# One decoder layer in fp32 on one core: subtractions moved to GpSimd, raw memory results, heads by the bank and x loaded ahead in a blocked-product kernel

## The chip, the core and the metric

The kernel runs on one core of one Trainium2 chip. A core has TensorE (PE, matrix products), VectorE (DVE), ScalarE (ACT) and GpSimd (POOL), which work side by side on tiles in SBUF, and PSUM banks of 128 x 512 fp32 values into which TensorE writes. Each engine takes its instructions in the order of its own queue. SyncE (SP) and GpSimd issue the DMA transfers. The metric is the device time of one execution in microseconds; less is better.

## The reference

One layer of a hybrid decoder: 512 tokens, width 2048, fp32. One normed input goes through one projection to three groups of heads, whose results are normed, gated and projected back; then follows a two-layer MLP with squared ReLU. Cut to what matters:

```python
def gla_chunked(q, k, v, log_a):          # 8 heads, 64 query/key and 128 value columns
    def step(state, xs):
        qi, ki, vi, gi = xs
        b = jnp.cumsum(gi, axis=2)
        inter = jnp.einsum('bhck,bhkv->bhcv', qi * jnp.exp(b), state)
        rel = b[:, :, :, None, :] - b[:, :, None, :, :]
        decay = jnp.exp(jnp.where(causal, rel, -jnp.inf))
        scores = jnp.einsum('bhik,bhijk,bhjk->bhij', qi, decay, ki)
        intra = jnp.einsum('bhij,bhjv->bhiv', scores, vi)
        ...

def reference(x, mem, ...):
    xn = rms_norm(h, attn_norm_g)
    proj = xn @ w_in
    (gq, gk, gv, gg, ga, fq, fk, fv, fg, ff, mq, mg) = jnp.split(proj, _split_points(), axis=-1)
    gla_o = gla_chunked(heads(gq), heads(gk), heads(gv), log_sigmoid(...) / 16)
    fox_o = forgetting_attention(rms_norm(fq), rms_norm(fk), fv, log_f)      # 4 heads, causal
    mk, mv = jnp.split(rms_norm(mem, mem_norm_g) @ w_mem_kv, 2, axis=-1)     # 256 memory tokens
    m_p = softmax(rms_norm(mq) . rms_norm(mk) / sqrt(128))
    mem_o = m_p . mv                                                          # 4 heads
    o = rms_norm(concatenate([gla_o, fox_o, mem_o]))
    gate = concatenate([silu(gg), sigmoid(fg), sigmoid(mg)])
    h = x + (o * gate) @ w_out
    u = relu(rms_norm(h, mlp_norm_g) @ w_up)
    return h + (u * u) @ w_down
```

## The kernel before

**Products.** Each fp32 matrix product is made of three matmuls in a reduced format (`mm3`, lines 154 to 156): the high half of one side by the high and the low half of the other, and the low half by the high. A block of weights comes by DMA, ScalarE casts it to its high half and VectorE subtracts that from it for the low half (line 370 in the blocked products, 146 and 147 in the plain projections).

**Blocked products.** Large projections are computed by the scheme of seven products for a 2 x 2 block matrix, in the order 1, 5, 6, 3, 7, 2, 4 (`multiply`, line 374). The right-hand sides for products 5, 6, 7 and 4 are differences of weight blocks. `Weights.prepare` makes them in place with `minus` (line 332, on VectorE), and `split` halves them. The left-hand sides (`left0` to `left6`) are sums of blocks of the activations. A product 6 adds to the accumulators of product 1, and so waits until the result of product 1 has been added to its part of the output. Three variants follow one another:

- `Pair` (lines 465 to 510): the projections gv and fq, fk, in four pairs in00, in01, in10 and in11 of seven products each, from 96 to 254 us. Its blocks are 128 x 1024, its `minus` (line 481) stands on GpSimd for products 7 and 4 and on VectorE for 5 and 6.
- `out0` and `out1` (from 735 to 910 us): the output projection. `out0` is the `w_first` of the code; its first splits are made while the last gates are. `block` (line 977) loads the part of x that a product is added to, `after` (line 988) adds the product to it.
- the MLP, up and down (910 to 2183 us), which the change leaves alone.

**Between the pairs and the output projection**, from 254 to 735 us, run the small projections, GLA, FoX (forgetting attention), memory attention and the gates. GLA takes the tokens in four chunks of 128. For each chunk it makes seven score groups, one for each level of halving (`lp_128` to `lp_2`): two differences of the cumulated decay against a reference row (lines 672 and 673, 128 x 256 each), an exponential on ScalarE, the products with queries (678) and keys (683), four matmuls (686) and a masked copy out of PSUM into the scores (690). Each level waits for the one step of each kind before it. Between them TensorE is fed with matmuls of fv, mq and the memory projection mkv, which the scheduler puts there. `attend` (line 402) is the softmax attention of FoX and memory, head by head.

**Order.** The program is written down in sequence and a scheduler orders each engine's instructions by priority: a block in `tc.high_priority(offset=...)` comes ahead by that amount. The weights use `AHEAD` = 3000, GLA uses 300, x of out0 and out1 uses 300. GpSimd's queue also carries the transfers of the left-hand sides to DRAM (`oo`, line 918), which are fetched back and halved anew (`resplit`, lines 858 and 859). The masks of GLA (`tri`, `suf`, `cmask`, `lmask`, lines 524 to 557) are built on GpSimd during the pairs.

Of the kernel before, what the change touches and what calls it, by code (L numbers as in the profile page):

```python
# [32 lines left out]
FH = 4  # L33
# [13 lines left out]
def hybrid_layer(  # L47
# [252 lines left out]
    class Weights:  # L300
# [30 lines left out]
        def minus(self, p, dst, a, b):  # L331
            V.tensor_sub(dst, a, b)  # L332
# [69 lines left out]
    def attend(n, logits, rowmax, v, dst, name):  # L402

        av = abank(f"av_{name}")
        sm = tp.tile([128, 4], F32, tag=f"sm{name[0]}", name=f"sm_{name}", bufs=2)
        nmx = tp.tile([128, 4], F32, tag="nmx", name=f"nmx_{name}", bufs=2)
        for h in range(4):
            lg = abank(f"lg_{name}_{h}")
            logits(h, lg)
            src = rowmax(h, lg, nmx[:, h : h + 1])  # L410
            p = tmp(f"p_{name}_{h}", "tb")
            A.activation(
                p[:, : n * 128], src[:, : n * 128], AF.Exp, bias=nmx[:, h : h + 1], accum_out=sm[:, h : h + 1]
            )
            pT = abank(f"pT_{name}_{h}")
            for s in range(n):
                T.transpose(pT[:, s * 128 : s * 128 + 128], p[:, s * 128 : s * 128 + 128], ident)
            pTs = tmp(f"pTs_{name}_{h}", "tc")
            A.copy(pTs[:, : n * 128], pT[:, : n * 128])
            for s in range(n):  # L420
                T.matmul(
                    av[:, h * 128 : h * 128 + 128], lhsT=pTs[:, s * 128 : s * 128 + 128], rhs=v(s, h),
                    start=s == 0, stop=s == n - 1,
                )
        rc = tp.tile([128, 4], F32, tag="hr", name=f"rc_{name}", bufs=4)
        V.reciprocal(rc, sm)
        V.tensor_mul(heads4(dst), heads4(av), rc.unsqueeze(2).broadcast_to([128, 4, 128]))
# [38 lines left out]
    class Pair(Weights):  # L466
# [13 lines left out]
        def minus(self, p, dst, a, b):  # L480
            (G if p in (7, 4) else V).tensor_tensor(dst, a, b, op=ALU.subtract)
# [143 lines left out]
    for ql in qls:  # L625
        G.memset(ql, 0.0)
    state = tmp("state", "rbx")
    fqT = bigt(2, [128, 4, S], "fqT")
    fkT = bigt(3, [128, 4, S], "fkT")
    with tc.high_priority(offset=GLA_AHEAD):  # L630
        for t in range(NT):
            normed_T(o[:, t, 1024:1536], g_fq, FOX_SCALE, fqT[:, :, t * 128 : t * 128 + 128], f"fq{t}")
        for c in range(NT):
# [31 lines left out]
            for li, B in enumerate(LEVELS):  # L665
# [6 lines left out]
                V.tensor_sub(ev[:, :, :hb], ref, bv[:, :, :hb])  # L672
                V.tensor_sub(ev[:, :, hb:], bv[:, :, hb:], ref)
# [33 lines left out]
            if c:  # L707
                qe = tmp(f"qe_{c}", "tc")
                V.tensor_mul(qe, qT, eb)
            ops = [abank(f"o_{c}_{i}") for i in range(2)]  # L710
            for h in range(GH):
                p, s = h // 2, (h % 2) * 64
                dst = ops[h % 2][:, p * 128 : p * 128 + 128]
                if c:
                    T.matmul(
                        dst, lhsT=qe[s : s + 64, p * 128 : p * 128 + 128],
                        rhs=state[s : s + 64, p * 128 : p * 128 + 128], start=True, stop=False,
                    )
                T.matmul(dst, lhsT=sc[:, h, :], rhs=o[:, c, h * 128 : h * 128 + 128], start=c == 0, stop=True)
# [31 lines left out]
    mqT = bigt(0, [128, 4, S], "mqT")  # L751
    for t in range(NT):
        scaled(o[:, t, 1536:2048], ps[t], rs_x(t), t)
        normed_T(o[:, t, 1536:2048], g_mq, FOX_SCALE, mqT[:, :, t * 128 : t * 128 + 128], f"mq{t}")

    mps = [[gbank(f"mkv_{m}_{n}") for n in range(2)] for m in range(MT)]

    room = spare[:, : 6 * M].rearrange("p (i m) -> p i m", m=M)
    macc = room[:, 0, :]
    for k in range(NK):  # L760
        with tc.high_priority(offset=AHEAD):
            mt = room[:, 1 + k % 3, :]
            nc.sync.dma_start(mt, memT[k])
            mh, ml = (tp.tile([128, M], FR, tag=f"mem{p}", name=f"mem{p}_{k}") for p in "hl")
            split_gain(mt, g_mem[:, k : k + 1], mh, ml)
            add_squares(macc, mt, k == 0, f"mem{k}", room[:, 4 + k % 2, :])
# [6 lines left out]

    with tc.high_priority(offset=AHEAD):
        mrstd = token_rstd(macc, MT, "mem")
# [4 lines left out]
    for m in range(MT):  # L780
        mk = tmp(f"raw_mk{m}", "ta")
        scaled(mk, mps[m][0], mrstd[:, m : m + 1], m)
        normed_T(mk, g_mk, 1.0, mkT[:, :, m * 128 : m * 128 + 128], f"mk{m}")
        with tc.high_priority(offset=AHEAD):
            A.activation(mv[:, m, :], mps[m][1], AF.Copy, scale=mrstd[:, m : m + 1])
# [21 lines left out]
    for t in reversed(range(NT)):  # L807
        n = (t + 1) * 128

        def fox_logits(h, lg, t=t, n=n):  # L810
            T.matmul(
                lg[:, :n], lhsT=fqT[:, h, t * 128 : t * 128 + 128], rhs=fkT[:, h, :n], start=True, stop=False
            )
            T.matmul(
                lg[:, :n], lhsT=negid[:, h : h + 1].broadcast_to([32 + FH, 128]), rhs=rows_r[:, :n],
# [3 lines left out]
        def fox_max(h, lg, nmx, t=t, n=n):  # L819
            ls = tmp(f"ls_{t}_{h}", "ta")  # L820
            V.tensor_tensor_reduce(
                ls[:, :n], lg[:, :n], cmask[:, S - n :], 1.0, 0.0, ALU.add, ALU.max, accum_out=nmx
            )
            V.tensor_scalar(nmx, nmx, -1.0, None, op0=ALU.mult)
            return ls
# [49 lines left out]
    def mem_max(h, lg, nmx):  # L875
        V.tensor_reduce(nmx, lg[:, :M], AX.X, ALU.max, negate=True)
        return lg

    for n, (group, silu) in enumerate(gates):
# [42 lines left out]
        if n == 0:  # L922
            with tc.high_priority(offset=AHEAD):
                for t in range(NT):
# [3 lines left out]
                            lg[:, :M], lhsT=mqT[:, h, t * 128 : t * 128 + 128], rhs=mkT[:, h, :], start=True, stop=True  # L928
# [45 lines left out]
    def out_pair(n):  # L974
        z, ht = {}, {}

        def block(r, c):

            with tc.high_priority(offset=300):
# [277 lines left out]
```

## Time and profile before

| | |
|---|---|
| median of three runs | 2185.28 us (2185.14 to 2186.91) |
| profiled execution: time, span | 2185.21 us, 2183.5 us |
| TensorE busy | 2126.2 us, 97% |
| VectorE, ScalarE, GpSimd busy | 1631.3, 1123.2, 213.0 us |
| TensorE's clock over the span | 0.993 of full speed |

A row of the profile's waits names who waited, for what, and gives total us, how often, and the longest. A row of the timeline gives the start and the length of an instruction in us, its engine, line, operation, and its output and inputs with their shapes; a last bracket is idle time ahead of it. A row of windows gives the width of a stretch, then for each engine the busy us (and instructions), the granted clock of TensorE, the DMA share and GB/s. Tile names stand without buffer numbers, so `raw_in` is any pair's weight block and `spare` a working area that holds others.

### The profile page before, as it was taken

What the parts mean: (1) busy time and instruction counts of PE and PEld (TensorE: products, weight loads), DVE (VectorE), ACT (ScalarE), POOL (GpSimd) and SP (SyncE); (2) the same over time, 40 slices, a digit from 0 to 9 for tenths busy, and PEclk for the clock granted to TensorE, in tenths of its full rate; (3) what the DMA queues carried; (4) which work ended last, traced back from release to release, by engine and by line L of the source; (5) the groups of instructions that cost most, each with busy time, mean ns of one, the idle gap of its engine ahead of it and who ended that gap; (6) DMA issues with size and microseconds to landing.
All of it is one profiled execution on the core that took longest, in us unless ns stands there. A gap on an engine that the chain in (4) does not pass through costs nothing.

```text
span 2183.5 us, 25488 instructions
## 1 busy us (share of the span) xinstructions
PE 2126.2 (97%) x9746; PEld 1728.5 (79%) x9746; DVE 1631.3 (75%) x1800; ACT 1123.2 (51%) x1535; POOL 213.0 (10%) x245
## 2 busy tenths in 40 slices
PE   8999999989999889999999999999999999999999
PEld 7887777767777668878888888888788788788787
DVE  6579977884666779887768768769868767877875
ACT  6454433344564545755554555556646545556443
POOL 1346100000000003100000000000000000000000
PEclk9999999999999989999999999999999999999999
DMA  7333211241213455533543443455577678668654
GB/s 269 102 118 112 87 59 49 88 143 39 88 61 132 180 217 212 211 117 141 177 144 137 167 168 120 162 182 193 195 219 203 183 202 248 168 191 253 182 167 131
DMA packets 74628, 339.24 MB, mean 155 GB/s; under 512 B 8633, under 2 KB 10681, under 8 KB 53002
## 3 DMA queue, kind: packets, MB, share of 16 engines
q1 hardware_dynamic: 55898, 270.76, 35.3%
q0 software_dynamic: 18608, 66.86, 11.7%
q8 instruction: 76, 1.25, 0.2%
q14 instruction: 46, 0.38, 0.1%
HBM read 266.54 MB, written 71.04 MB: 155 GB/s over the span
## 4 chain that ended last, share of the span: by engine, by line
PE 78%; DVE 11%; DMA 4%; issue 3%; ACT 2%; POOL 1%; SPq 0%; DVEq 0%; ACTq 0%; POOLq 0%
PE acc_up L154 9%; PE acc_up L155 9%; PE acc_up L156 9%; PE acc_dn L155 7%; PE acc_dn L156 7%; PE acc_dn L154 7%; PE acc_out L154 2%; PE acc_out L155 2%; PE acc_out L156 2%; DMA left1l<-op 2%; DVE hl_dn L370 1%; DVE raw_dn L332 1%; DMA left5l<-op 1%; PE gg L154 1%; PE ut L1072 1%
## 5 line engine op out<-in xcount | busy, mean ns | idle before, releaser
L370 DVE TENSOR_TENSOR hl_up<-raw_up,hl_up 128x1024 fp32r<-128x1024 f32 x224 | 271.6, 1221 | 141.6 <-ACT hl_up L370 141.5
L370 ACT CAST hl_up<-raw_up 128x1024 fp32r<-128x1024 f32 x224 | 235.3, 1052 | 253.7 <-PE acc_up L156 193.9
L370 DVE TENSOR_TENSOR hl_dn<-raw_dn,hl_dn 128x1024 fp32r<-128x1024 f32 x224 | 270.5, 1221 | 99.5 <-ACT hl_dn L370 98.7
L370 ACT CAST hl_dn<-raw_dn 128x1024 fp32r<-128x1024 f32 x224 | 234.4, 1053 | 204.6 <-PE acc_dn L156 163.5
L332 DVE TENSOR_TENSOR raw_dn<-raw_dn,raw_dn 128x2048 f32<-128x2048 f32 x64 | 146.1, 2286 | 16.1 <-DMA raw_dn<-in_w_down_dram 15.9
L332 DVE TENSOR_TENSOR raw_up<-raw_up,raw_up 128x2048 f32<-128x2048 f32 x64 | 145.1, 2267 | 1.4 <-DMA raw_up<-in_w_up_dram 1.3
L370 ACT CAST hl_out<-raw_out 128x1024 fp32r<-128x1024 f32 x56 | 58.7, 1052 | 68.6 <-PE acc_out L156 55.3
L1172 POOL DMA_DIRECT2D hd<-m x48 | 41.0, 854 | 516.1 <-ACT m L1171 516.1
L370 DVE TENSOR_TENSOR hl_out<-raw_out,hl_out 128x1024 fp32r<-128x1024 f32 x56 | 69.2, 1253 | 25.0 <-ACT hl_out L370 25.0
L1171 ACT COPY m<-acc_dn 128x512 f32<-128x512 f32 x96 | 54.5, 587 | 30.3 <-PE acc_dn L156 30.3
L1064 POOL DMA_DIRECT2D op<-u x32 | 17.1, 534 | 486.3 <-ACT u L1073 479.1
L370 DVE TENSOR_TENSOR hl_hl_in<-spare,hl_hl_in 128x1024 fp32r<-128x1024 f32 x31 | 45.6, 1481 | 15.6 <-ACT hl_hl_in L370 15.6
L154 PE MATMUL gg<-ahi_x,hl_gg 128*128 128x512 f32 x128 | 54.6, 427 | 2.6 <-ACT raw_mk L222 2.2
L370 ACT CAST hl_hl_in<-spare 128x1024 fp32r<-128x1024 f32 x31 | 32.5, 1049 | 43.4 <-PE acc_in L156 18.9
L155 PE MATMUL acc_dn<-hl_dn,left 128*128 128x512 f32 x128 | 50.3, 393 | 4.6 <-DVE hl_dn L370 4.6
L155 PE MATMUL gg<-alo_x,hl_gg 128*128 128x512 f32 x128 | 53.7, 419 | 0.0
L156 PE MATMUL gg<-ahi_x,hl_gg 128*128 128x512 f32 x128 | 53.2, 415 | 0.0
L154 PE MATMUL acc_up<-hl_up,left 128*128 128x512 f32 x128 | 49.9, 390 | 3.1 <-ACT z L1127 3.1
L155 PE MATMUL acc_in<-hl_hl_in,sh 128*128 128x512 f32 x128 | 50.2, 392 | 2.6 <-DVE hl_hl_in L370 2.6
L155 PE MATMUL acc_dn<-hl_dn,left0h 128*128 128x512 f32 x128 | 50.2, 392 | 1.2 <-DVE hl_dn L370 1.2
L154 PE MATMUL acc_in<-hl_hl_in,sh 128*128 128x512 f32 x128 | 49.9, 390 | 0.7 <-DVE o L499 0.7
L155 PE MATMUL acc_dn<-hl_dn,left3h 128*128 128x512 f32 x128 | 50.5, 395 | 0.0
(566 smaller groups left out, 6320.0 us busy)
## 6 DMA issues: line engine op xcount, KB each, us to landing
raw_up<-in_w_up_dram SPq DMA_DIRECT2D x64, 1024.0 KB, 4.8
raw_dn<-in_w_down_dram SPq DMA_DIRECT2D x64, 1024.0 KB, 6.8
hd<-m POOLq DMA_DIRECT2D x48, 512.0 KB, 5.6
raw_out<-in_w_out_dram SPq DMA_DIRECT2D x16, 1024.0 KB, 5.7
op<-u POOLq DMA_DIRECT2D x32, 512.0 KB, 3.8
op<-s POOLq DMA_DIRECT2D x24, 512.0 KB, 2.9
spare<-in_w_pair_dram SPq DMA_DIRECT2D x16, 512.0 KB, 4.3
raw_in<-in_w_pair_dram SPq DMA_DIRECT2D x16, 512.0 KB, 3.6
```

The lines of the kernel that those rows point to most:

```text
L154: T.matmul(ps, lhsT=ah, rhs=bh, start=start, stop=False, skip_group_check=on)
L155: T.matmul(ps, lhsT=ah, rhs=bl, start=False, stop=False, skip_group_check=on)
L156: T.matmul(ps, lhsT=al, rhs=bh, start=False, stop=stop, skip_group_check=on)
L332: V.tensor_sub(dst, a, b)
L370: made = A.copy(hi, part), V.tensor_sub(lo, part, hi.bitcast(F32))
L1064: nc.gpsimd.dma_start(down_op[c][i][:, half * 1024 : half * 1024 + 1024], tile)
L1072: T.transpose(tps[:, m * 128 : m * 128 + 128], z[:, t * 512 + m * 128 : t * 512 + m * 128 + 128], ident)
L1171: A.copy(st[:, t * 512 : t * 512 + 512], acc[t])
L1172: nc.gpsimd.dma_start(dst, st.rearrange("p (t n) -> p t n", t=2), accum_op=ALU.add)
```

## The change

Seven edits in one.

1. The differences for product 5 of the pairs go from VectorE to GpSimd, so that GpSimd has 5, 7 and 4.
2. In `out0`, the differences for products 7 and 4 go from VectorE to GpSimd.
3. GLA's two differences a level go from VectorE to GpSimd.
4. The queries that GLA multiplies with the state are written into a zeroed tile with one head's rows and zeros in the other's, and the matmul takes all 128 rows.
5. The results of the memory projection are copied out of PSUM unscaled, with their scale applied after; the norms of the memory queries come after the memory keys' instead of before the projection.
6. `attend` takes as many heads at once as fit in a bank: one exponential per head still, but one maximum, one copy and one transposed bank for 2 to 4 heads in the small blocks.
7. The parts of x for `out0` are loaded at priority 3 x AHEAD instead of 300.

```diff
         def minus(self, p, dst, a, b):
-            V.tensor_sub(dst, a, b)
+            (G if self.name == "out0" and p in (7, 4) else V).tensor_tensor(dst, a, b, op=ALU.subtract)
...
-        for h in range(4):
-            lg = abank(f"lg_{name}_{h}")
-            logits(h, lg)
-            src = rowmax(h, lg, nmx[:, h : h + 1])
+        m, b = n * 128, 4 // n
+        for h0 in range(0, 4, b):
+            lg = abank(f"lg_{name}_{h0}")
+            for i in range(b):
+                logits(h0 + i, lg[:, i * m : i * m + m])
+            src = rowmax(h0, b, lg, nmx[:, h0 : h0 + b])
...
         def minus(self, p, dst, a, b):
-            (G if p in (7, 4) else V).tensor_tensor(dst, a, b, op=ALU.subtract)
+            (G if p in (5, 7, 4) else V).tensor_tensor(dst, a, b, op=ALU.subtract)
...
+    qz = spare[:, 5 * M : 9 * M].rearrange("p (h s t) -> p h s t", h=4, s=2)
+    mraw = spare[:, 9 * M : 13 * M].rearrange("p (m c) -> p m c", m=MT)
+    G.memset(qz, 0.0)
...
-                V.tensor_sub(ev[:, :, :hb], ref, bv[:, :, :hb])
-                V.tensor_sub(ev[:, :, hb:], bv[:, :, hb:], ref)
+                G.tensor_tensor(ev[:, :, :hb], ref, bv[:, :, :hb], op=ALU.subtract)
+                G.tensor_tensor(ev[:, :, hb:], bv[:, :, hb:], ref, op=ALU.subtract)
...
             if c:
-                qe = tmp(f"qe_{c}", "tc")
-                V.tensor_mul(qe, qT, eb)
+                for s in range(2):
+                    rows = slice(s * 64, s * 64 + 64)
+                    V.tensor_mul(qz[rows, :, s, :], heads4(qT)[rows], heads4(eb)[rows])
...
-        normed_T(o[:, t, 1536:2048], g_mq, FOX_SCALE, mqT[:, :, t * 128 : t * 128 + 128], f"mq{t}")
...
     with tc.high_priority(offset=AHEAD):
+        for m in range(MT):
+            V.tensor_copy(mks[:, m, :], mps[m][0])
+            A.copy(mraw[:, m, :], mps[m][1])
         mrstd = token_rstd(macc, MT, "mem")
...
-        scaled(mk, mps[m][0], mrstd[:, m : m + 1], m)
+        V.tensor_scalar(mk, mks[:, m, :], mrstd[:, m : m + 1], None, op0=ALU.mult)
         normed_T(mk, g_mk, 1.0, mkT[:, :, m * 128 : m * 128 + 128], f"mk{m}")
...
+    for t in range(NT):
+        normed_T(o[:, t, 1536:2048], g_mq, FOX_SCALE, mqT[:, :, t * 128 : t * 128 + 128], f"mq{t}")
...
-            with tc.high_priority(offset=300):
+            with tc.high_priority(offset=300 if n else 3 * AHEAD):
                 z[r, c] = stage(f"x_{n}_{r}{c}")
                 nc.sync.dma_start(z[r, c].rearrange("p (t n) -> p t n", t=2), x[r, 2 * n + c])
```

How the change moves instructions is best seen in three places. The lines of the changed program are a few higher than those of before (672 and 673 are 682 and 683, 686 is 696, 481 is 485, 859 is 873, 988 is 1002).

First, GpSimd's queue in the third pair, in10. Before, after the pairs' sums, it held the rest of the masks, and then the differences for product 7 (`raw_in_110`, `raw_in_111`):

```order
L556 AFFINE_SELECT lmask<-lmask 128x64 x3
L557 AFFINE_SELECT lmask<-lmask 128x64 x3
L556 AFFINE_SELECT lmask<-lmask 128x64 x3
L557 AFFINE_SELECT lmask<-lmask 128x64 x3
L556 AFFINE_SELECT lmask<-lmask 128x64
L597 MEMSET rows_v 17x512
L557 AFFINE_SELECT lmask<-lmask 128x64
L481 TENSOR_TENSOR spare<-raw_in_110_1460,spare 128x1024
L481 TENSOR_TENSOR spare<-raw_in_111_1463,spare 128x1024
```

After, two subtractions for product 5 (with the outputs `raw_in_000`, and `spare` from `spare` alone) stand among the masks:

```order
L560 AFFINE_SELECT lmask<-lmask 128x64
L485 TENSOR_TENSOR raw_in_000_1387<-spare,raw_in_000_1387 128x1024
L561 AFFINE_SELECT lmask<-lmask 128x64
L560 AFFINE_SELECT lmask<-lmask 128x64
L485 TENSOR_TENSOR spare<-raw_in_110_1460,spare 128x1024
L561 AFFINE_SELECT lmask<-lmask 128x64
L560 AFFINE_SELECT lmask<-lmask 128x64 x3
L561 AFFINE_SELECT lmask<-lmask 128x64 x3
L560 AFFINE_SELECT lmask<-lmask 128x64 x2
L601 MEMSET rows_v 17x512
L485 TENSOR_TENSOR spare<-spare 128x1024
```

Of the masks one stands ahead of the first of them and eleven, with a memset and the product 7 subtraction, between it and the second.

Second, TensorE's queue in GLA's first chunk. Before, eleven matmuls of fv stand between the score groups of level 16 and level 8:

```order
L155 MATMUL fv_2870<-hl_fv_3018,ahi_x_505 128x512
L156 MATMUL fv_2870<-hl_fv_3018,alo_x_506 128x512
L154 MATMUL fv_2871<-hl_fv_3018,ahi_x_505 128x512
L155 MATMUL fv_2871<-hl_fv_3018,ahi_x_505 128x512
L156 MATMUL fv_2871<-hl_fv_3018,alo_x_506 128x512
L154 MATMUL fv_2868<-hl_fv_3018,ahi_x_526 128x512
L155 MATMUL fv_2868<-hl_fv_3018,ahi_x_526 128x512
L156 MATMUL fv_2868<-hl_fv_3018,alo_x_527 128x512
L154 MATMUL fv_2869<-hl_fv_3018,ahi_x_526 128x512
L155 MATMUL fv_2869<-hl_fv_3018,ahi_x_526 128x512
L156 MATMUL fv_2869<-hl_fv_3018,alo_x_527 128x512
L686 MATMUL lp_8_2226<-ql_2041,e_8_2219 128x128 x4
```

After, two stand between them:

```order
L696 MATMUL lp_16_2214<-ql_2042,e_16_2207 128x128 x4
L155 MATMUL fv_2872<-hl_fv_2990,ahi_x_450 128x512
L156 MATMUL fv_2872<-hl_fv_2990,alo_x_451 128x512
L696 MATMUL lp_8_2227<-ql_2041,e_8_2220 128x128 x4
L154 MATMUL fv_2869<-hl_fv_3019,ahi_x_505 128x512
```

Over a chunk's seven groups there are 57, 57, 60 and 130 projection matmuls before, and 34, 32, 36 and 34 after; the rest stand between the chunks or, for the last one, behind it.

Third, VectorE's queue in `out0`, from product 6's splits on. Before, a subtraction for product 7 (`raw_out_011`; that of `raw_out_010` stands right ahead of these rows) and the resplits of the left-hand sides stood ahead of the additions into x (`x_00`):

```order
L370 TENSOR_TENSOR hl_out_62_6195<-raw_out_001_5894,hl_out_62_6195 128x1024
L370 TENSOR_TENSOR hl_out_63_6210<-raw_out_001_5894,hl_out_63_6210 128x1024
L332 TENSOR_TENSOR raw_out_011_6072<-raw_out_111_6160,raw_out_011_6072 128x2048
L859 TENSOR_TENSOR left4m<-left4m,left_4282 128x512
L859 TENSOR_TENSOR left6l<-left6l,left6h 128x1536
L859 TENSOR_TENSOR left6l<-left6l,left6h 128x512
L859 TENSOR_TENSOR left5l<-left5l,left5h 128x1536
L859 TENSOR_TENSOR left5l<-left5l,left5h 128x512
L859 TENSOR_TENSOR left1l<-left1l,left1h 128x1536
L859 TENSOR_TENSOR left1l<-left1l,left1h 128x512
L988 TENSOR_TENSOR x_00_6041<-x_00_6041,acc_out_1_0_6027 128x512
L988 TENSOR_TENSOR x_00_6041<-x_00_6041,acc_out_1_1_6028 128x512
```

After, the additions follow the third split of product 6:

```order
L370 TENSOR_TENSOR hl_out_53_6057<-raw_out_001_5811,hl_out_53_6057 128x1024
L370 TENSOR_TENSOR hl_out_60_6080<-raw_out_000_5809,hl_out_60_6080 128x1024
L332 TENSOR_TENSOR raw_out_001_5811<-raw_out_111_6077,raw_out_001_5811 128x2048
L370 TENSOR_TENSOR hl_out_61_6097<-raw_out_000_5809,hl_out_61_6097 128x1024
L370 TENSOR_TENSOR hl_out_62_6112<-raw_out_001_5811,hl_out_62_6112 128x1024
L1002 TENSOR_TENSOR x_00_5958<-x_00_5958,acc_out_1_0_5944 128x512
L1002 TENSOR_TENSOR x_00_5958<-x_00_5958,acc_out_1_1_5945 128x512
L1002 TENSOR_TENSOR x_11_6007<-x_11_6007,acc_out_5_0_5984 128x512
L1002 TENSOR_TENSOR x_11_6007<-x_11_6007,acc_out_5_1_5985 128x512
L370 TENSOR_TENSOR hl_out_63_6127<-raw_out_001_5811,hl_out_63_6127 128x1024
L873 TENSOR_TENSOR left4m<-left4m,left_4247 128x512
L370 TENSOR_TENSOR hl_out_30_6144<-raw_out_110_6074,hl_out_30_6144 128x1024
```

And on GpSimd the two subtractions for product 7 stand around the fence and ahead of the last transfers of left-hand sides to DRAM:

```order
L932 DMA oo_4254<-s_fg 128x512
L332 TENSOR_TENSOR raw_out_010_5986<-raw_out_110_6074,raw_out_010_5986 128x2048
L952 MEMSET fence 128x56
L332 TENSOR_TENSOR raw_out_011_5989<-raw_out_111_6077,raw_out_011_5989 128x2048
L932 DMA oo_4249<-o 128x2x256
L932 DMA oo_4250<-o 128x2x256
L932 DMA oo_4253<-s_mg 128x512
L932 DMA oo_4252<-s_mg 128x512
L932 DMA oo_4254<-s_mg 128x512
```

82 lines of the change are left out of this document (43 added, 39 removed).

## The prediction

> **What bounds the kernel now.** I read the busy shares first, then the idle time of TensorE by what ended it, then busy time by stretches of the program.
>
> ```profile
> PE 2126.2 (97%) x9746; PEld 1728.5 (79%) x9746; DVE 1631.3 (75%) x1800; ACT 1123.2 (51%) x1535; POOL 213.0 (10%) x245
> ```
> ```profile
> PE acc_out L154 <- DVE x L988: 14.5, 1, 14.5
> ...
> PE lp L686 <- DVE e L683: 4.1, 12, 0.6
> ...
> PE tps_mq L237 <- DVE nrm_mq L230: 3.0, 2, 2.0
> ...
> PE gg L154 <- ACT raw_mk L222: 2.2, 1, 2.2
> ...
> PE acc_out L154 <- ACT left3h L915: 2.0, 1, 2.0
> ```
>
> TensorE is busy in 2126.2 of 2183.5 us, so the kernel is a chain of matmuls with 57 us of holes. No edit takes matmul work away in any amount, so the change is worth what it fills of these holes, less the holes that it opens. The columns of the second fence are total us, count and longest. The largest hole, 14.5 us, is one wait of out0 for the addition into x. The scores of GLA (lp) wait 4.1 us, and the end of the memory projection 3.0 and 2.2 us. Together 23.8 us stand where the change works.
>
> ```profile
> start us, us, engine line op out<-in xcount [idle before <-releaser]
> 152.55 0.73 POOL L280 TENSOR_TENSOR st<-xs,xs 128x256 f32<-128x256 f32 x1
> ...
> 158.28 1.71 POOL L280 TENSOR_TENSOR st<-xs,xs 128x256 f32<-128x256 f32 x1
> ...
> 195.69 2.40 POOL L481 TENSOR_TENSOR raw_in<-raw_in,raw_in 128x1024 f32<-128x1024 f32 x1 [1.17 <-DVE hl_hl_in L370]
> 198.07 3.36 POOL L481 TENSOR_TENSOR spare<-raw_in,spare 128x1024 f32<-128x1024 f32 x1
> ```
> ```profile
> 195.54 1.40 DVE L499 SCALAR_TENSOR_TENSOR o<-acc_in,r_x,o 128x512 f32<-128x512 f32 x2
> ...
> 199.09 3.42 DVE L370 TENSOR_TENSOR hl_hl_in<-raw_in,hl_hl_in 128x1024 fp32r<-128x1024 f32 x1
> ...
> 212.07 1.21 DVE L370 TENSOR_TENSOR hl_hl_in<-spare,hl_hl_in 128x1024 fp32r<-128x1024 f32 x1
> ```
>
> The change gives GpSimd subtractions that VectorE made, so I look at how the two engines run side by side. GpSimd's 128x1024 subtraction takes 2.40 us and VectorE's 1.21 us when each runs alone. From 198.07 to 201.43 both have one, and the two take 3.36 and 3.42 us: about the sum of the prices, so one stood while the other ran. The same with the small form, 0.73 us alone and 1.71 beside VectorE. An operation with one input in PSUM (L499, 0.70 us each) ran at its price beside GpSimd's 2.40 us. So **work moved from VectorE to GpSimd doesn't leave VectorE's time: it comes back as twice the blocking**, wherever VectorE's own operations read two tiles of SBUF.
>
> **The change part by part.** The sum is made against the profiled execution, 2185.21 us, which is the median shown (2185.28) within 0.1 us; its span is 2183.5.
>
> Product 5 of the pairs. Eight subtractions go to GpSimd. In the third pair (in10, the rows above) they enter GpSimd's queue between the masks, as the order shows.
>
> ```profile
> 174.06 1.22 DVE L481 TENSOR_TENSOR raw_in<-spare,raw_in 128x1024 f32<-128x1024 f32 x1
> ...
> 177.68 1.26 DVE L370 TENSOR_TENSOR hl_hl_in<-raw_in,hl_hl_in 128x1024 fp32r<-128x1024 f32 x1
> ...
> 180.12 1.26 DVE L370 TENSOR_TENSOR hl_hl_in<-spare,hl_hl_in 128x1024 fp32r<-128x1024 f32 x1
> ```
> ```profile
> 175.36 1.06 ACT L370 CAST hl_hl_in<-raw_in 128x1024 fp32r<-128x1024 f32 x1 [2.12 <-DVE raw_in L481]
> ```
> ```profile
> 175.69 3.37 POOL L556 TENSOR_SCALAR_AFFINE_SELECT lmask<-lmask 128x64 f32<-128x64 f32 x3
> ...
> 182.71 1.96 POOL L556 TENSOR_SCALAR_AFFINE_SELECT lmask<-lmask 128x64 f32<-128x64 f32 x3
> ...
> 188.01 0.52 POOL L597 MEMSET rows_v<- 17x512 f32 x1
> ```
> ```profile
> 179.46 0.39 PE L155 MATMUL acc_in<-hl_hl_in,sh 128*128 128x512 f32 x1
> ...
> 182.18 0.39 PE L155 MATMUL acc_in<-hl_hl_in,sh 128*128 128x512 f32 x1
> ```
>
> Before, the low halves for product 5 were ready at 178.94 and 181.38, and TensorE used them at 179.46 and 182.18: 0.5 and 0.8 us of slack. Now the first subtraction follows one mask row (to 175.69 + 1.12 = 176.8) and ends at 179.2; cast 1.06 and split 1.26 make 181.5, 2 us late. The second stands behind two more mask rows (2 x 1.1, to 181.4), the product-7 subtraction (2.40, to 183.8), nine mask rows (0.65 each at the pace of 182.71, 5.9, to 189.7) and a memset (0.5): it runs from 190.2 to 192.6, and its low half is there at 194.9. That is 194.9 - 182.2 = 12.7 us late. Some comes back: the later subtractions have then got ahead, and that pair's small waits fall away, which I put at 2 us. The other pairs' rows have no masks ahead, at about 0. **+10.5 us**; bounds: +3, if the masks stall only the first half, to +13.
>
> GLA. Fifty-six differences per program (14 a chunk of 128 tokens) move to GpSimd.
>
> ```profile
> L683 DVE TENSOR_TENSOR e<-e,kTs 128x512 f32<-128x512 f32 x28 | 19.6, 702 | 0.0
> ...
> L673 DVE TENSOR_TENSOR e<-bT 128x256 f32<-128x256 f32 x28 | 12.3, 438 | 0.3
> L672 DVE TENSOR_TENSOR e<-bT 128x256 f32<-128x256 f32 x28 | 11.8, 421 | 4.6 <-ACT bT L651 4.4
> ```
> ```profile
> L690 DVE COPY_PREDICATED scores<-lmask,lp 128x512 f32<-128x512 int32 x28 | 24.9, 889 | 2.9 <-PE lp L686 2.8
> ```
> ```profile
> 294.30:321.40 27.10, 25.64 (x141) 20.56 (x140) 25.16 (x47) 8.32 (x12) 1.29 (x1) 1.00 0.18 62
> 330.40:357.90 27.50, 26.09 (x146) 21.12 (x145) 26.68 (x50) 10.52 (x16) 1.76 (x1) 1.00 0.20 61
> ```
>
> These windows (columns: width, then busy time of PE, its weight load, DVE, ACT, POOL) are two chunks, from the first difference to the first matmul on the finished scores. VectorE is busy 25.2 of 27.1 us, TensorE 25.6. The moved work is 14 x 0.43 = 6.0 us of VectorE and becomes 14 x 0.73 = 10.2 us of GpSimd, which VectorE must mostly stand aside for: 25.2 - 6.0 + 10.2 = 29.4 us if nothing overlaps. What can overlap is L690, whose scores come from PSUM, 7 x 0.889 = 6.2 us; with all of it beside GpSimd 23.2 remain. I take 25, nearer the low end, because L499 showed such an operation run free. Meanwhile the order gives the chunk less to do on TensorE: 34 projection matmuls between its seven score groups in place of 57, and 23 x 0.23 (the pace of the rows at 179) = 5.3 us leave. So 25.6 - 5.3 = 20.3 us of work stand in 25: 4.7 us idle a chunk. Four chunks make 18.8, less the 4.1 us of today: **+14.5 us**. Bounds: -4, if the lock hides in gaps and the waits vanish, to 4 x 9.1 - 4.1 = +32.
>
> The Trainium skill, "SBUF — State Buffer", section "Who interferes with whom", says that a VectorE instruction with two SBUF inputs and a GpSimd instruction that reads SBUF exclude each other for the whole instruction, while one with at most one SBUF input doesn't contend. The mask of L690 is one SBUF input and its other comes from PSUM, so by that rule 23.2 us would do, an idle of 2.9 us a chunk and +7.5 us; counted the other way, with L690 blocked too, it would be +32. The trace agrees on L499 (0.70 us) and on L370 (3.42).
>
> ```profile
> L719 PE MATMUL o<-o,scores 128*128 128x128 f32 x64 | 12.9, 307 | 0.0
> L715 PE MATMUL o<-state,qe 64*128 64x128 f32 x48 | 10.7, 322 | 0.0
> ```
> ```profile
> L709 DVE TENSOR_TENSOR qe<-qTs,eb 128x512 f32<-128x512 f32 x3 | 2.0, 680 | 0.0
> ```
>
> Zero-filled queries: six half-height products (256 columns, 0.42 us as L672) for three of 0.68, and matmuls over 128 rows for 64, which cost the same (307 and 322 ns). 0, at most +1.
>
> Memory results raw, query norms behind them. The transposes that waited (3.0 us) go behind the projection, and the wait of 2.2 us for the scaled keys falls, since the banks are emptied unscaled.
>
> ```profile
> 489.40:494.20 4.80, 4.79 (x11) 3.80 (x12) 3.12 (x12) 4.57 (x12) 0.00 (x0) 0.51 0.01 3
> ```
>
> After the holes the granted clock was 0.51 for 4.8 us, in which 11 matmuls ran that take 11 x 0.23 = 2.5 at pace: 2.3 more. 3.0 + 2.2 + 2.3 = 7.5; the copies that empty the banks are now the last to be waited for, at 1.5. **-6 us**; bounds -7.5 and 0. FoX and memory heads by the bank shorten VectorE and ScalarE chains that nobody waits for there: 0.
>
> x of out0 loaded ahead, and its products 7 and 4 subtracted on GpSimd.
>
> ```profile
> 736.16 1.23 DVE L332 TENSOR_TENSOR raw_out<-raw_out,raw_out 128x1024 f32<-128x1024 f32 x1 [1.77 <-DMA raw_out<-in_w_out_dram]
> ...
> 759.50 2.28 DVE L332 TENSOR_TENSOR raw_out<-raw_out,raw_out 128x2048 f32<-128x2048 f32 x1
> ...
> 766.17 0.68 DVE L859 TENSOR_TENSOR left4m<-left4m,left 128x512 fp32r<-128x512 f32 x1
> ...
> 773.59 1.28 DVE L988 TENSOR_TENSOR x<-x,acc_out 128x512 f32<-128x512 f32 x2
> ```
> ```profile
> 759.20:774.30 15.10, 0.60 (x2) 0.00 (x0) 15.10 (x14) 9.91 (x11) 0.00 (x0) 0.61 0.96 380
> ```
>
> From 736.16 to 773.59 VectorE works almost without a pause (15.10 of 15.10 us in the hole itself), and the addition stands last. The change takes out two L332 (2 x 2.28) and puts the resplits from 766.17 to 773.59 (7.4 us) and one split (1.2) behind the addition: 13.2 us. But GpSimd's 128x2048 subtraction, estimated from 0.73 us for 256 columns and 2.40 for 1024 (2.17 ns a column, so 2.40 + 1024 x 2.17 ns = 4.6 us), comes twice ahead of the addition and blocks VectorE: +9.2. The addition is 4.0 us earlier: **-4 us**. Product 4's two come after it, where TensorE has no wait today: 0. Bounds: -16.6 with no blocking (the wait of 14.5 whole, and about 2.1 of slow clock, as after the hole at 489), +2 if the memory copies to DRAM, which queue behind the second subtraction on GpSimd, come late for product 3.
>
> Sum: 2185.2 + 10.5 + 14.5 - 6 - 4 = 2200.2, **2200 us**.
>
> **The rivals.** First, *GpSimd's work fits into VectorE's gaps* and the scheduler's tighter packing pays: GLA -4, out0 -16.6, memory -7.5, pairs +10.5: 2167.6, faster. For it: VectorE has 25% idle over the span. Against it: in these very stretches it has 7% or none. It decides if VectorE's splits keep 1.22 us there. Second, *the gains are whole and the locks cost as I say*: 10.5 + 14.5 - 7.5 - 16.6 = +0.9, 2186; this needs out0's two long subtractions to fall where VectorE waits, and it waits only 1.8 us at 736. Third, *blocking takes L690 in too*, or the short-run differences cost 1.71 as at 158.28: 10.5 + 32 - 6 - 4 = +32.5, 2218. A further form, that product 5 alone costs nothing because the masks are early, shifts each by -10 and lies in the range.
>
> **How the numbers follow.** Forecast (2193 to 2210) 0.45; first rival (2160 to 2180) 0.22; second (2180 to 2193) 0.15; third (2210 to 2230) 0.18. The measurement of this kernel can tell about 0.2%, 4.4 us, from no change: below 2180.9 lie the first rival and 0.01 of the second, within lie 0.09, above the rest. The range 2172 to 2220 leaves out 0.12 below and 0.08 above.
>
> **What would show it.** Right: a wait of TensorE of some 12 us in the third pair for L370's split; splits of 2 to 4 us beside GpSimd in GLA, and lp waits near 19 us; no wait for the memory norms; the wait for x near 10 us, GpSimd at 4.6 us each ahead. Wrong: lp waits under 4 us, x's under 3, or differences over 1.2 us on GpSimd.

## The result, and the profile after

| | before | changed |
|---|---|---|
| median | 2185.21 us (4 runs, 2182.19 to 2186.91) | 2197.36 us (4 runs, 2194.72 to 2199.20) |
| ratio, 95% interval | | 1.0056, 1.0039 to 1.0074 |
| span of the profiled execution | 2183.5 us | 2196.7 us |
| TensorE busy | 2126.2 us | 2126.9 us |

The change makes the kernel 12 us slower; 2200 was forecast. TensorE's work is the same, and its idle time grew from 57 to 70 us. The waits of the changed kernel (total us, times, longest) show where:

```profile
PE lp L696 <- DVE e L693: 15.3, 14, 2.5
PE acc_out L155 <- DVE hl_out L370: 10.9, 4, 5.6
PE acc_in L155 <- DVE hl_hl_in L370: 6.0, 3, 2.5
...
PE acc_out L154 <- ACT left3h L929: 3.6, 1, 3.6
PE acc_in L154 <- ACT hl_hl_in L370: 3.5, 1, 3.5
...
PE fg L154 <- DVE z_gg L915: 2.6, 1, 2.6
PE acc_out L154 <- DVE x L1002: 1.7, 1, 1.7
```

The wait for x in `out0` is gone but for 1.7 of 14.5 us, and those at the end of the memory projection are gone. In their place stand the score groups with 15.3 instead of 4.1, splits of `out0` with 10.9 instead of 2.1, and the pairs with 9.5 instead of 2.8. Five stretches of the program, cut where TensorE begins the pairs, the small projections, the gates, fg, the output projections and the MLP, first before and then changed (the second column is the width):

```profile
95.70:254.00 158.30, 154.27 (x674) 125.61 (x674) 132.88 (x123) 73.60 (x88) 66.39 (x47) 1.00 0.32 107
254.00:489.40 235.40, 225.65 (x1171) 171.58 (x1169) 192.15 (x412) 91.83 (x163) 8.95 (x7) 1.00 0.24 82
489.40:637.40 148.00, 147.61 (x728) 112.11 (x729) 77.98 (x203) 75.49 (x178) 2.80 (x4) 0.98 0.18 61
637.40:731.50 94.10, 91.82 (x418) 75.09 (x417) 59.58 (x111) 48.45 (x83) 5.15 (x8) 1.00 0.36 123
731.50:913.40 181.90, 163.21 (x730) 133.97 (x728) 151.95 (x136) 105.16 (x153) 33.80 (x39) 0.94 0.61 225
```
```profile
95.80:263.40 167.60, 157.54 (x674) 127.92 (x674) 133.43 (x118) 73.10 (x88) 75.60 (x55) 0.97 0.31 100
263.40:497.10 233.70, 217.33 (x1156) 171.55 (x1155) 178.86 (x327) 88.76 (x149) 50.36 (x63) 0.99 0.25 79
497.10:644.10 147.00, 146.78 (x746) 112.66 (x744) 87.57 (x209) 77.80 (x179) 2.81 (x4) 1.00 0.20 69
644.10:739.90 95.80, 91.73 (x416) 75.14 (x417) 60.02 (x114) 48.91 (x83) 5.16 (x8) 1.00 0.35 121
739.90:925.10 185.20, 167.99 (x730) 136.13 (x729) 160.52 (x132) 104.97 (x153) 59.53 (x43) 0.94 0.61 221
```

The widths differ by +9.3, -1.7, -1.0, +1.7 and +3.3 us, 11.6 of the 13.2 us between the spans. Most of the rest is in the MLP (1270.1 and 1271.6 us), whose instructions didn't change; over the profiles of this study it takes 1267.9 to 1271.6 us. Below, the five are called pairs, middle, gates, fg and out.

**The pairs.** GpSimd's and VectorE's rows of the third pair:

```profile
176.44 2.39 POOL L485 TENSOR_TENSOR raw_in<-spare,raw_in 128x1024 f32<-128x1024 f32 x1
...
179.19 2.37 POOL L485 TENSOR_TENSOR spare<-raw_in,spare 128x1024 f32<-128x1024 f32 x1
...
187.02 2.34 POOL L485 TENSOR_TENSOR spare<-spare 128x1024 f32<-128x1024 f32 x1
```
```profile
179.96 2.69 DVE L370 TENSOR_TENSOR hl_hl_in<-raw_in,hl_hl_in 128x1024 fp32r<-128x1024 f32 x1 [3.58 <-ACT hl_hl_in L370]
...
190.47 3.31 DVE L370 TENSOR_TENSOR hl_hl_in<-spare,hl_hl_in 128x1024 fp32r<-128x1024 f32 x1 [6.56 <-ACT hl_hl_in L370]
```

```profile
190.49 0.80 PE L154 MATMUL acc_in<-hl_hl_in,sh 128*128 128x512 f32 x1 [3.49 <-ACT hl_hl_in L370]
```

The second subtraction for product 5 starts at 187.02, behind the masks, and the split after it ends at 193.8. VectorE and TensorE had both been waiting.

**GLA.** VectorE's rows in the middle, before and then changed:

```profile
L678 DVE TENSOR_TENSOR ql<-qTs,e 64x256 f32<-64x256 f32 x56 | 24.4, 435 | 0.6
```
```profile
L688 DVE TENSOR_TENSOR ql<-qTs,e 64x256 f32<-64x256 f32 x56 | 32.8, 585 | 2.7 <-ACT e L684 1.9
L700 DVE COPY_PREDICATED scores<-lmask,lp 128x512 f32<-128x512 int32 x28 | 25.0, 892 | 1.9 <-PE lp L696 1.1
...
L147 DVE TENSOR_TENSOR hl_mq<-raw_mq,hl_mq 128x1024 fp32r<-128x1024 f32 x8 | 10.3, 1284 | 5.2 <-ACT hl_mq L146 5.2
```

The products with the queries last 585 ns instead of 435, but the masked copy keeps its time (892 and 889 ns), and the splits of mq nearly so (1284 and 1221 ns). The chunks, from the first difference to the first matmul on the scores, take 24.1, 24.8, 25.1 and 27.9 us, where they took 27.4, 27.8, 27.6 and 47.9 with more projection matmuls in them. In the first, TensorE is busy for 20.5 of 24.1 us and VectorE for 21.9.

**out0.** A row of VectorE before, its rows after, and GpSimd's four subtractions:

```profile
737.30 3.49 DVE L370 TENSOR_TENSOR hl_out<-raw_out,hl_out 128x1024 fp32r<-128x1024 f32 x3
```
```profile
745.74 7.92 DVE L370 TENSOR_TENSOR hl_out<-raw_out,hl_out 128x1024 fp32r<-128x1024 f32 x3
...
765.27 5.00 DVE L930 TENSOR_TENSOR left3l<-s_mg,left3h 128x512 fp32r<-128x512 f32 x1
...
777.65 1.28 DVE L1002 TENSOR_TENSOR x<-x,acc_out 128x512 f32<-128x512 f32 x2
...
802.23 5.54 DVE L370 TENSOR_TENSOR hl_out<-raw_out,hl_out 128x1024 fp32r<-128x1024 f32 x1
```
```profile
747.35 5.22 POOL L332 TENSOR_TENSOR raw_out<-raw_out,raw_out 128x2048 f32<-128x2048 f32 x1 [35.45 <-DMA raw_out<-in_w_out_dram]
...
760.88 8.85 POOL L332 TENSOR_TENSOR raw_out<-raw_out,raw_out 128x2048 f32<-128x2048 f32 x1 [2.07 <-DVE raw_out L365]
...
794.42 5.67 POOL L332 TENSOR_TENSOR raw_out<-raw_out,raw_out 128x2048 f32<-128x2048 f32 x1 [21.64 <-DMA raw_out<-in_w_out_dram]
800.69 6.00 POOL L332 TENSOR_TENSOR raw_out<-raw_out,raw_out 128x2048 f32<-128x2048 f32 x1 [0.60 <-DVE left5l L873]
```

Three splits of 128x1024 that took 3.49 us together take 7.92 beside GpSimd's first subtraction. A split of 128x512, 0.68 us when alone, lasts 5.00 us while the second runs, and one of 128x1024 lasts 5.54 beside the fourth. The second subtraction itself takes 8.85 us, where the first took 5.22; VectorE's instructions beside its first half kept their usual times. The addition into x starts 37.75 us after the stage does, where it started 42.1 us after before. TensorE stands idle for 3.6 us up to 765.25 and for 5.6 us up to 772.06, ahead of this addition, and for 4.4 us up to 807.8, behind the fourth subtraction.

### The profile page after: what moved, and what is told of

Same layout as the page of the kernel before. It is cut to its first block, busy times and chain, and to the rows that moved or that the text cites. A ratio compares the mean times of both kernels' runs of the same rounds, so it can differ in the third digit from the quotient of the medians.

```text
span 2196.7 us, 25468 instructions
## 1 busy us (share of the span) xinstructions
PE 2126.9 (97%) x9746; PEld 1734.9 (79%) x9746; DVE 1636.1 (74%) x1712; ACT 1122.5 (51%) x1523; POOL 295.8 (13%) x314
## 4 chain that ended last, share of the span: by engine, by line
PE 80%; DVE 10%; issue 4%; DMA 3%; ACT 2%; POOL 2%; SPq 0%; ACTq 0%; POOLq 0%; DVEq 0%
PE acc_up L154 9%; PE acc_up L155 9%; PE acc_up L156 9%; PE acc_dn L155 7%; PE acc_dn L156 7%; PE acc_dn L154 7%; PE acc_out L155 2%; PE acc_out L154 2%; PE acc_out L156 2%; DMA left1l<-op 2%; DVE hl_dn L370 1%; PE acc_in L155 1%; PE acc_in L156 1%; DVE raw_dn L332 1%; PE acc_in L154 1%
## 5 line engine op out<-in xcount | busy, mean ns | idle before, releaser
L370 DVE TENSOR_TENSOR hl_out<-raw_out,hl_out 128x1024 fp32r<-128x1024 f32 x56 | 77.9, 1409 | 18.4 <-ACT hl_out L370 18.4
L370 DVE TENSOR_TENSOR hl_hl_in<-spare,hl_hl_in 128x1024 fp32r<-128x1024 f32 x31 | 49.5, 1602 | 22.0 <-ACT hl_hl_in L370 21.9
L370 DVE TENSOR_TENSOR hl_hl_in<-raw_in,hl_hl_in 128x1024 fp32r<-128x1024 f32 x25 | 45.2, 1814 | 9.9 <-ACT hl_hl_in L370 9.5
```

The lines of the kernel that those rows point to most:

```text
L370: made = A.copy(hi, part), V.tensor_sub(lo, part, hi.bitcast(F32))
```

## The experiments

Each run is a version of the changed kernel unless said otherwise. Times are medians, with the ratio to the kernel before the change, measured beside it; widths of stretches are from the profiles.

### Product 5 of one pair back on VectorE, aimed wrongly

```diff
-            (G if p in (5, 7, 4) else V).tensor_tensor(dst, a, b, op=ALU.subtract)
+            (G if p in (7, 4) or p == 5 and self.name != "in10" else V).tensor_tensor(dst, a, b, op=ALU.subtract)
```

> The changed kernel with product 5 of the third pair (in10) alone back on VectorE; the six other subtractions for product 5 stay on GpSimd. My theory, the queue: the loss in the pairs is the place of in10's two subtractions among the masks on GpSimd. Then TensorE's waits in that pair (2.2 and 6.0 us) go and the kernel is 8 to 10 us faster than the changed one, about 2188. Rival, the lock: each of the eight subtractions costs by blocking VectorE. Then two of eight bring back a quarter of 9 us, about 2.3, and the kernel stands near 2195.

2198.23 us, 1.0067 (1.0049 to 1.0085), the pairs again 167.6 us wide. The loops run the pairs as in00, in10, in01, in11, so that in10 is the second pair. The third, with the masks, is in01, though the prediction and the text ahead of it call it in10. The miss still says something: two subtractions that stand on GpSimd away from the masks cost nothing that shows in the width.

### Product 5 wholly on VectorE

```diff
-            (G if p in (5, 7, 4) else V).tensor_tensor(dst, a, b, op=ALU.subtract)
+            (G if p in (7, 4) else V).tensor_tensor(dst, a, b, op=ALU.subtract)
```

> The changed kernel with all subtractions for product 5 of the pairs back on VectorE. Both theories on the pairs: about 9 us less than the changed kernel, 2188; the pairs take 158.5 us as before the change. If it equals the run with in10 alone on VectorE, the other six subtractions on GpSimd cost nothing.

2189.47 us, 1.0024 (1.0014 to 1.0033). The pairs are 158.3 us wide, as before the change.

### Product 5 of the third pair on VectorE

```diff
-            (G if p in (5, 7, 4) else V).tensor_tensor(dst, a, b, op=ALU.subtract)
+            (G if p in (7, 4) or p == 5 and self.name != "in01" else V).tensor_tensor(dst, a, b, op=ALU.subtract)
```

> The changed kernel with product 5 of the third pair alone back on VectorE (the code calls that pair in01; the run named after in10 moved the second pair's two subtractions instead, and changed nothing). Queue theory: TensorE's waits of 2.2 and 6.0 us go, and the pairs take 158.5 us, all of the 9.2 us that the run with product 5 wholly on VectorE brought, though six subtractions stay on GpSimd: 2188. Rival, the lock in every pair: a quarter of it, 2195.

2189.24 us, 1.0019 (1.0010 to 1.0029). The stretch of the pairs:

```profile
97.00:254.80 157.80, 154.55 (x674) 125.52 (x675) 135.54 (x119) 72.98 (x88) 79.27 (x52) 1.00 0.33 106
```

All of it comes back with two subtractions of eight. What the pairs lose is a place in a queue, not the lock (VectorE and GpSimd standing still for each other).

### GLA's differences on VectorE

```diff
-                G.tensor_tensor(ev[:, :, :hb], ref, bv[:, :, :hb], op=ALU.subtract)
-                G.tensor_tensor(ev[:, :, hb:], bv[:, :, hb:], ref, op=ALU.subtract)
+                V.tensor_sub(ev[:, :, :hb], ref, bv[:, :, :hb])
+                V.tensor_sub(ev[:, :, hb:], bv[:, :, hb:], ref)
```

> The changed kernel with GLA's differences back on VectorE. My theory: GpSimd's differences block VectorE, and the tighter packing leaves TensorE without filling; undone, the waits for the score groups (16.4 us) fall to about 4.5 and the kernel is 12 us faster, about 2185. Rival: the chunk is shorter with GpSimd's help (24.1 us from the first difference to the first matmul on the scores, against 27.1), and VectorE becomes the late one again, so that only 4 us or less come back, 2193 or more.

2182.57 us, 0.9992 (0.9983 to 1.0002). The middle falls to 221.7 us, 12.0 less, as the theory had it, and the waits for scores are 3.9 us. The rest of the gain stands in out, 179.6 instead of 185.2, where this run changed nothing; out with GpSimd's four subtractions took between 179.6 and 187.8 us in the profiles of this study, and which of VectorE's instructions they fall on differs between them.

### out0's products 7 and 4 on VectorE

```diff
-            (G if self.name == "out0" and p in (7, 4) else V).tensor_tensor(dst, a, b, op=ALU.subtract)
+            V.tensor_tensor(dst, a, b, op=ALU.subtract)
```

> The changed kernel with the subtractions for products 7 and 4 of out0 back on VectorE; x is still loaded ahead. My theory: GpSimd's four subtractions of 5 to 9 us each block VectorE; without them the addition into x is 5 us earlier, product 7's wait of 4.4 us and the slow clock behind it go, and the output projections take 173 us instead of 185: 12 us less, about 2185. Rival: VectorE then has 9 us more of its own, and the resplits of the left-hand sides, which stand behind the addition, become the wait: 4 us less at most, 2193.

2183.91 us, 0.9994 (0.9984 to 1.0003).

```profile
740.50:910.70 170.20, 162.89 (x729) 133.69 (x728) 151.44 (x136) 104.93 (x153) 33.84 (x39) 0.98 0.66 241
```

Out takes 170.2 us: 15.0 less than changed, and 11.7 less than before the change. This is what loading x ahead is worth when nothing takes it back: TensorE's wait for x is 3.1 us here and was 14.5 before the change. No run undoes that edit alone.

### out0's product 4 alone on VectorE

```diff
-            (G if self.name == "out0" and p in (7, 4) else V).tensor_tensor(dst, a, b, op=ALU.subtract)
+            (G if self.name == "out0" and p == 7 else V).tensor_tensor(dst, a, b, op=ALU.subtract)
```

> The changed kernel with the two subtractions for out0's product 4 back on VectorE, those for product 7 on GpSimd as changed. My theory: product 4's two, put at nothing in the prediction, block a split of product 7 (5.5 us) and make TensorE wait 4.4 us with slow clock behind it; undone, the output projections take about 178 us instead of 185.2. Rival: the wait has another cause, and the stage stays above 183.

2191.33 us, 1.0033 (1.0021 to 1.0045); out is 177.8 us wide, 7.4 less than changed, and the ratio falls by 0.0023, about 5 us. So about a third to a half of GpSimd's cost in out0 was product 4's, in these two profiles. The cost depends on where the two fall: in the run with GLA's differences on VectorE they are still on GpSimd, and yet that wait of TensorE is 1.0 us instead of 4.4 and out takes 179.6 us.

### No GpSimd subtractions added

Product 5 wholly, GLA's differences and out0's products 7 and 4 all back on VectorE; x ahead, zero-filled queries, raw memory results and heads by the bank stay.

> The changed kernel with all three kinds of subtraction back on VectorE; the four other edits stay. The three gains measured one by one, 9.2 in the pairs, 12.0 in GLA and 15.0 in out0, stand in different stages and should add up: 36 us less than the changed kernel, about 2161, 24 us or 1.1% less than before the change. Rival: they share VectorE, so that what one gives back the next takes; then less than 28 us, 2169 or more.

2160.40 us, **0.9888 (0.9873 to 0.9903)**: 1.1% faster than before the change, and 37 us less than the changed kernel. The three gains (36.2 us by the profiles) add up within about a microsecond. What TensorE still waits for:

```profile
PE lp L696 <- DVE e L693: 3.9, 10, 1.1
...
PE acc_out L154 <- DVE x L1002: 3.1, 1, 3.1
PE acc_in L155 <- DVE hl_hl_in L370: 2.9, 4, 1.2
```

### The zero-filled queries undone as well

```diff
-                for s in range(2):
-                    rows = slice(s * 64, s * 64 + 64)
-                    V.tensor_mul(qz[rows, :, s, :], heads4(qT)[rows], heads4(eb)[rows])
+                qe = tmp(f"qe_{c}", "tc")
+                V.tensor_mul(qe, qT, eb)
...
-                    T.matmul(dst, lhsT=qz[:, p, s, :], rhs=state[:, p * 128 : p * 128 + 128], start=True, stop=False)
+                    T.matmul(
+                        dst, lhsT=qe[s * 64 : s * 64 + 64, p * 128 : p * 128 + 128],
+                        rhs=state[s * 64 : s * 64 + 64, p * 128 : p * 128 + 128], start=True, stop=False,
+                    )
```

> As the run without GpSimd's subtractions, and with the zero-filled queries undone too: the matmuls on the state take 64 rows again. My theory: 64-row and 128-row matmuls in turn cost TensorE more than their durations show (24 of them took 5.0 us in the second chunk before, 0.21 each, against 0.11 where all are of 128 rows), so this run is 6 to 7 us slower than that one, 2168. Rival, my prediction: 0.

2166.06 us, 0.9912 (0.9896 to 0.9927), 5.7 us slower than with the zero-filled queries by medians of four runs each, which spread over 5 and 7 us. In the profiles the middle is 4.5 us wider, and fg 1.4. TensorE's timeline shows it, in the second chunk before the change and after it:

```profile
359.96 0.49 PE L719 MATMUL o<-o,scores 128*128 128x128 f32 x2
360.37 0.48 PE L715 MATMUL o<-state,qe 64*128 64x128 f32 x2
360.79 0.49 PE L719 MATMUL o<-o,scores 128*128 128x128 f32 x2
361.21 0.49 PE L715 MATMUL o<-state,qe 64*128 64x128 f32 x2
```
```profile
362.37 0.39 PE L727 MATMUL o<-o,scores 128*128 128x128 f32 x2
362.59 0.39 PE L726 MATMUL o<-state,spare 128*128 128x128 f32 x2
362.81 0.39 PE L727 MATMUL o<-o,scores 128*128 128x128 f32 x2
```

Where 64-row and 128-row pairs alternate, one pair starts 0.42 us after the other; where all have 128 rows, 0.22 us. The run with 64 rows has the 0.42 us again, at the full granted clock.

### GpSimd's differences for nobody

To the kernel of the run without added GpSimd subtractions, GLA's 56 are added on GpSimd, into a place that nobody reads. TensorE's, VectorE's and ScalarE's work stays as it was.

```diff
+                idle = spare[:, 13 * M :].rearrange("p (n b) -> p n b", b=hb)
+                G.tensor_tensor(idle, ref, bv[:, :, :hb], op=ALU.subtract)
+                G.tensor_tensor(idle, bv[:, :, hb:], ref, op=ALU.subtract)
```

> The run without GpSimd's subtractions, with GLA's differences made twice: VectorE's are used as before, and GpSimd makes the same 56 into a place that nobody reads. No instruction of another engine moves and none waits for them. Lock theory: VectorE stands aside for part of 56 x 0.62 us; its products with the queries, 425 ns there, get longer, the waits for the score groups rise, and the kernel is 10 us or more slower than that run, 2170 or above. Rival, the longer way: in the changed kernel it is the extra engine between decay and exponential that costs; then work that nobody waits for changes less than 3 us, 2160 to 2163.

2177.32 us, 0.9973 (0.9963 to 0.9983). The middle is 239.2 us wide, 17.4 more. VectorE's groups in it, without these differences and with them:

```profile
L700 DVE COPY_PREDICATED scores<-lmask,lp 128x512 f32<-128x512 int32 x28 | 24.9, 888 | 3.1 <-PE lp L696 3.0
L688 DVE TENSOR_TENSOR ql<-qTs,e 64x256 f32<-64x256 f32 x56 | 23.8, 425 | 0.6
...
L683 DVE TENSOR_TENSOR e<-bT 128x256 f32<-128x256 f32 x28 | 12.9, 460 | 0.2
L682 DVE TENSOR_TENSOR e<-bT 128x256 f32<-128x256 f32 x28 | 11.8, 420 | 4.6 <-ACT bT L661 4.5
```
```profile
L691 DVE TENSOR_TENSOR ql<-qTs,e 64x256 f32<-64x256 f32 x56 | 29.8, 532 | 0.6
L703 DVE COPY_PREDICATED scores<-lmask,lp 128x512 f32<-128x512 int32 x28 | 24.8, 887 | 3.1 <-PE lp L699 3.0
...
L683 DVE TENSOR_TENSOR e<-bT 128x256 f32<-128x256 f32 x28 | 16.5, 590 | 0.2
L682 DVE TENSOR_TENSOR e<-bT 128x256 f32<-128x256 f32 x28 | 15.9, 569 | 4.7 <-ACT bT L661 4.5
```

The same instructions of VectorE take 25 to 35% longer with GpSimd's beside them; the masked copy out of PSUM (887 ns, 888 without) does not. Between a chunk's score groups stand as many projection matmuls as without them (57, 57, 62 and 143), and the four chunks are 4.4 to 4.8 us longer each. No instruction needs the added work: the profile does put two waits of a weight load (4.8 us) down to it, but both loads start 0.1 us after VectorE's product for them ends. So the lock alone makes these 17 us.

### More filling in two chunks

```diff
-GLA_AHEAD = 300
+GLA_AHEAD = 150
```

> The changed kernel with GLA's priority at 150 instead of 300: the differences stay on GpSimd, but the scheduler leaves 62 and 84 projection matmuls between the score groups of the third and fourth chunk, where the changed kernel has 36 and 34; the first two chunks keep 34 and 32. Packing theory: the waits come from too little filling in a chunk; in the third and fourth chunk they fall from 9.0 us to about 2, and the kernel is 7 us faster than the changed one, 2190, with the lock still there. Lock theory: VectorE's blocked time makes the chunk longer by as much, and the waits stay within 2 us, 2196.

2200.48 us, 1.0069 (1.0053 to 1.0086). The middle is 233.2 us wide, against 233.7: the packing theory falls. The waits for scores went from 15.3 to 12.9 us; in the third and fourth chunk together they went from 8.9 to 6.6, where the theory had about 2, and these chunks grew from 25.1 and 27.9 to 30.6 and 39.1 us. The stretch grew no shorter.

### More buffers for the differences

```diff
-                e = tmp(f"e_{name}", "ta")
+                e = tmp(f"e_{name}", "ta" if li % 2 else "tc")
```

> The changed kernel with the tile of the differences taken in turn from two sets of three buffers, so that six levels can be under way instead of three. Buffer theory: GpSimd stands 25 us waiting for the score matmuls of an earlier level to free a tile; with six the waits for the score groups (16.4 us) fall below 9 and the stretch from the small projections to the gates takes 226 us or less instead of 233.6. Lock theory: the waits stay at 13 us or more and the stretch at 230 or more.

2208.44 us, 1.0108 (1.0088 to 1.0127), the slowest of all. The middle takes 245.2 us and the waits for scores are 23.1 us. The buffer theory falls. It isn't the lock that grew, though: VectorE's products with the queries last 567 ns, against 585. What grew is VectorE's wait for ScalarE's casts, to 10.3 us from 5.2 in the case of mq:

```profile
L147 DVE TENSOR_TENSOR hl_mq<-raw_mq,hl_mq 128x1024 fp32r<-128x1024 f32 x8 | 10.4, 1299 | 10.3 <-ACT hl_mq L146 10.3
```

In the fourth chunk GpSimd makes its fourteen differences one after another, six of ScalarE's exponentials stand ahead of a cast, and VectorE idles 3.9 us for that cast while TensorE waits 4.5. That this order makes the whole 11.5 us isn't shown.

### Half of the differences on GpSimd

```diff
-                G.tensor_tensor(ev[:, :, hb:], bv[:, :, hb:], ref, op=ALU.subtract)
+                V.tensor_sub(ev[:, :, hb:], bv[:, :, hb:], ref)
```

> The changed kernel with only the first of the two differences of each level on GpSimd, the second on VectorE. Lock theory: half of the blocking, so about half of the 12 us comes back: 227.5 us from the small projections to the gates instead of 233.6, the kernel near 2191. Rival, the longer way: each level still waits for GpSimd, and most of the loss stays, 231 us or more.

2186.55 us, 1.0013 (1.0003 to 1.0023).

```profile
264.30:486.50 222.20, 214.44 (x1156) 168.21 (x1155) 179.00 (x355) 88.19 (x149) 30.82 (x35) 1.00 0.26 83
```
```profile
L688 DVE TENSOR_TENSOR ql<-qTs,e 64x256 f32<-64x256 f32 x56 | 24.7, 441 | 1.2 <-ACT e L684 0.4
```

Neither theory foresaw this. The middle takes 222.2 us, and VectorE's products 441 ns: nearly all of the 12 us is back, with 28 differences still on GpSimd. A loss in proportion to the moved work doesn't give this. With each engine on one half of a level's differences, GpSimd's last 853 ns and VectorE's 539 (460 without GpSimd's), and the products behind them keep their time. But the run changes more than the blocked work: between a chunk's score groups stand 44, 47, 44 and 62 projection matmuls, against 34, 32, 36 and 34 in the changed kernel, and both differences of a level are made side by side instead of one after the other. Which of the three brings the time back, and whether some share of the differences on GpSimd would be a gain, stays open.

## Why the prediction was right, and where it was not

The total came out within 3 us (2200 against 2197), and the sign and the main mechanism held. That it came so close is partly luck: GLA, memory and the queries came out lower than forecast and out0 and fg higher, and these errors cancelled. Two terms are also 0.2 us less than their own working gives (12.7 less 2 is 10.7, and 18.8 less 4.1 is 14.7), which changes nothing.

- **Product 5, +10.5: right.** +9.3, and the run with in01 alone shows that it is the masks' queue. The other pairs, at 0, were right too.
- **GLA, +14.5: right in size, and in cause as far as the runs show.** Undoing it gave 12.0. The chunks last 24 to 28 us, where 25 was taken, and TensorE's work in the first is 20.5 us, where 20.3 was. VectorE's 25 is not borne out: it is busy for 21.9 us there and waits for the rest. That the lock costs time was argued from four rows, and is shown by the differences that nobody reads, at an unchanged order. How the 12.0 us divide between the lock and the longer way, on which every exponential waits for GpSimd, no run separates, and the half speaks against a loss in proportion. The masked copy, whose scores come from PSUM, kept its 887 ns beside GpSimd. This agrees with the Trainium skill ("SBUF — State Buffer", section "Who interferes with whom"), by which a VectorE instruction with at most one SBUF input doesn't contend with GpSimd.
- **Zero-filled queries, 0: mis-sized.** The step "matmuls over 128 rows for 64, which cost the same (307 and 322 ns)" read an instruction's duration, not the distance between starts. Measured alone it is -5.7 us by medians and -4.5 in the middle.
- **Memory results and heads by the bank, -6 and 0: short, unless fg belongs to them.** The kernel with only these and x ahead differs from before by -9.1 us in the middle and -1.0 in the gates. The waits of 5.2 us and the slow clock behind them went as forecast, without the new wait of 1.5 us. Which of the two edits gives the rest wasn't tried. Against it stands fg, which is 4.6 us longer in that kernel: its wait for z_gg grew from 0.8 to 2.6 us, and the granted clock is 0.97 instead of 1.00. All versions of the changed kernel that were profiled have this stretch longer, and which edit makes it is open.
- **out0, -4: right for x, wrong for product 4.** The addition into x came 4.3 us earlier (4.0 forecast), and the two subtractions ahead of it cost VectorE 4.4 and 4.3 us (4.6 each forecast). "Product 4's two come after it, where TensorE has no wait today: 0" failed: they blocked a split of product 7, which went from 1.2 to 5.5 us, and cost 5 to 7 us there. A place without a wait has slack only for the durations that it has now. The stage came out at +3.3.
- **Not in the sum:** fg, 1.7 us longer in the changed kernel, and 1.5 us in the MLP, which is within the spread of its width over the profiles.

Some of the signs named ahead didn't come. The wait for x is 1.7 us, not near 10, and under 3 was to mean that the forecast is wrong: the addition came as early as said, but TensorE had just stood idle for 3.6 and 5.6 us (2.0 and 1.8 before the change) behind delayed splits, so that less was left to wait for. GLA's splits didn't grow to 2 to 4 us; they kept 1.2 to 1.3, and the small products took the blocking instead. So the splits, by which the first rival was to be decided, were the wrong rows to look at.

Of the rivals, the first, in which GpSimd's work fits into gaps, is out by the time: 2167.6 was its sum, and the kernel came to 2197. With the added subtractions back on VectorE it takes 2160.

## What to carry to other kernels

Before work goes from VectorE to GpSimd, see whether VectorE's neighbours there read two SBUF tiles. In this kernel they did, and their times grew: 56 differences that nobody reads cost 17 us, in chunks where VectorE is nearly always busy, though GpSimd is idle for most of the span. It isn't a fixed price, since half of the differences on GpSimd cost that stretch next to nothing. Look also at what stands in the queue of the engine that takes the work: two subtractions among masks cost nine microseconds, and six elsewhere cost none. When a change bundles edits, price and undo each by its stage: here four of seven were worth 25 us together, and the three others took away 37.

## What was not expected of the hardware

Small matmuls that alternate between 64 and 128 rows start 0.21 us apart, against 0.11 where all have 128 rows, though the durations in the profile differ far less (322 and 307 ns, against 280 and 279). Filling the 48 of 64 rows with zeros gained 4.5 us in their stretch of the profile and 5.7 us by the medians.
